# Strassen steps added in three units, two joins given to transfers, and another order of the branch units, in a one-core decoder block

## The chip, the cores and the metric

The kernel runs on one core of a Trainium2 chip. Its engines are TensorE (PE: matmuls, PEld: the weight loads that overlap them), VectorE (DVE), ScalarE (ACT), GpSimd (POOL, which here builds masks and issues transfers) and SyncE (SP, which only issues transfers). The metric is the device time of one execution in microseconds; "span" is the time from the first to the last instruction that the hardware profiler recorded.

## The reference

The block reads x (256 tokens × 4096 channels), normalizes it, multiplies it by one wide matrix and feeds two mixers, a causal pooling one and a gated short convolution. Each mixer's result goes through a branch matrix, is gated by a sigmoid, and the sum goes through an output matrix.

```python
h = rmsnorm(x, norm_w[l])
proj = jnp.einsum('bsd,de->bse', h, w_in[l])          # 4096 -> 20480
u_p, z_p, u_c, b_c, c_c, z_c, g_logit = jnp.split(proj, SPLIT_POINTS, axis=-1)
y_pool = causal_multiscale_pool(u_p, pool_w[l], pool_scale[l]) * jax.nn.silu(z_p)
y_conv = causal_gated_shortconv(u_c, b_c, c_c, conv_w[l], conv_b[l]) * jax.nn.silu(z_c)
ys = jnp.stack([y_pool, y_conv], axis=2)
br = jnp.einsum('bsnc,ncd->bsnd', ys, w_branch[l])    # 2 x (2048 -> 4096)
gates = jax.nn.sigmoid(g_logit.reshape(b, s, N_BRANCHES, d) + gate_b[l])
merged = jnp.sum(gates * br, axis=2)
x = x + jnp.einsum('bsd,de->bse', merged, w_out[l])   # 4096 -> 4096
return rmsnorm(x, final_norm_w)
```

## The kernel before

**Units and steps.** The work is a list of units, each of which makes 256 tokens × 1024 output columns. The eight units of the convolution come first (cz0, cb0, cu0, cc0, then the same with 1), then four of the pooling (pz0, pu0, pz1, pu1), eight of gate logits (g0_0 to g1_0), eight of the branch matrices (b0_0, b1_0, b0_1, ...; the first digit is the branch n, the second the column block c) and four of the output matrix (o0 to o3). A unit over x has 16 steps, one for each 256 input channels; a branch unit has 8. A step takes one 1 MB block of weights (256 channels × 1024 columns).

**Direct and Strassen steps.** Precision is kept by writing every fp32 operand as a high part, rounded to the matmul's format, and a low part, the rest; each product is three matmuls (high × high, high × low, low × high). A direct step, P, has 2 token halves × 2 column halves × 2 channel halves = 8 such products, 24 matmuls. A Strassen step, S, forms the sums of its weights' quarters on VectorE (tile `parts`) and needs 7 products, 21 matmuls. A string such as `"PPPPPSPSPSPSPSPS"` says which steps of a unit are which.

**What a step costs beside its matmuls.** SP loads the block into one of three `raw` buffers. ScalarE casts it to the high parts in a ring of 15 cells (`highs`, L58), VectorE subtracts to get the low parts (`lows`, L61). For an S step VectorE also adds the four weight sums, ScalarE casts them and VectorE subtracts once more (`added` and `split`). Up to `AHEAD = 4` steps are prepared ahead of the one that PE works on; a unit marked `urgent` sets this to its `lead` (2, or 3 for branch units) while its last step runs.

**The end of a unit.** Sums stand in eight PSUM banks: four `sums` banks (E) and four `shared` ones (F) that only S steps use. ScalarE copies each E bank out when its last matmul is done (`evacuate`, to E or Y) and each F bank to J. Where the unit has S steps, VectorE forms corner sums in J (`corner_sums`) and `combine` joins J to E: by a VectorE add, or, where the unit is marked `late`, by two accumulating transfers from the POOL queue (`gather`). The unit's epilogue `epi` is a list of items of which one runs for every six matmuls of the units behind it (`TICK = 6`).

**The order.** Everything is recorded in one pass and kept in program order on each engine, so an instruction waits for all that stands ahead of it on its engine. The queues of SP and POOL are filled in the same order.

**The first unit.** cz0 works while x is still being read and normalized: its 16 steps are all direct. VectorE and ScalarE each square one half of every block of rows (`square`), the scale of the tokens (`rin`) is known only near its end, and its E banks are copied to Y with that scale.

**The branch units.** b0_c leaves its product with the gates in Y, and b1_c multiplies by its own gates (`spare()`, the tile last_pair), adds Y, turns the sum by PE transposes (L462) and stores it to m_d for the output units. The operands of the branches (`y_ops`) are filled from y_d while earlier units run (`queue_fills`, `Fill`), in the order b0_0's, then b1_0's.

Of the kernel before, what the change touches and what calls it, by code (L numbers as in the profile page):

```python
# [31 lines left out]
TAIL = 3  # L32

SIX5 = "PPPPPSPSPSPSPSPS"
FIRST = (0, 1, 8, 2, 9, 3, 10, 11, 4, 12, 13, 5, 14, 6, 15, 7)
OPENED = 12
SEVEN3 = "PPPSPSPSPSPSPSPS"
NINE = "PSPSPSPSSPSPSSPS"
NINE_A = "PSPSSPSPSSPSPSPS"
NINE_P = "PSPSSPSPSSPSSPSP"  # L40
HOST = "PPBPPMMPSSPSSPSSPSS"
TEN = "PSPSSPSSPSSPSSPS"
OUT3 = "PSPSPSPSPSPSSPPP"
B0 = "PPPPSPSP"
B1 = "PSPSPSPP"
B1_FIRST = "PPSPSPSP"
B0_MORE = "PPPPSSPS"


@with_exitstack  # L50
def hybrid_block(ctx: ExitStack, tc: tile.TileContext, x, xc, prm, rows_in, w_in, pool_w, w_branch, w_out, out):
# [5 lines left out]
    def act(dst, src, func=AF.Copy, **kw):  # L57
        return pin(nc.scalar.activation(dst, src, func, **kw))  # L58
# [22 lines left out]
    def move(dst, src):  # L81
        return pin(nc.gpsimd.dma_start(dst, src))
# [36 lines left out]
    g_d = dram.tile([2, P, 2, NU], F32, name="g_d")  # L119
    side_d = dram.tile([2, P, 2, 4, P], F32R, name="side_d")  # L120
    y_d = dram.tile([2, 2, P, 4, 2, T], F32, name="y_d")
    m_d = dram.tile([4, P, 4, 2, T], F32, name="m_d")
    o_d = dram.tile([3, P, 2, NU], F32, name="o_d")

# [11 lines left out]
    def scale_col(b):  # L136
        return par[:, 96 + b:97 + b]

    opening = ExitStack()
    ctx.enter_context(opening)  # L140
    op = opening.enter_context(tc.tile_pool(name="opening", bufs=1))
# [313 lines left out]
    def transposes(src, done):  # L455
        items = []
        for j in range(4):
            def f(j=j):
                for i in range(2):
                    for t in range(2):  # L460
                        c = (2 * j + i) * P
                        pin(nc.tensor.transpose(shared(j)[:, i * T + t * P:i * T + (t + 1) * P],  # L462
                                                src[:, t, c:c + P], ident))
# [17 lines left out]
    def gap(n):  # L481
        return [None] * n
# [22 lines left out]

    def seq_x(text):
        if text is FIRST:
            return [("P", i) for i in FIRST]
        ns = text.count("S")
        if ns > NS + NB:  # L510
            ss = list(range(ND, 16)) + [resident[0]]
            if ns > NS + NB + 1:
                resident[0] = 2 * ND - 3 - resident[0]
                ss = [ss[-1]] + ss[:-1] + [resident[0]]
            ps = [i for i in range(ND) if i not in ss]
            return [(c, (ss if c == "S" else ps).pop(0)) for c in text]
        return sequence(text, ND, ND + NS + NB, NB)
# [4 lines left out]
    def in_unit(name, col, epi, text, **kw):  # L522
        units.append(Unit(name, lambda i: w_in[col // NU, i], seq_x(text), x_ops, epi, scaled=True, **kw))
        units[-1].text = text
        return units[-1]
# [12 lines left out]
            lambda: sub(side["tile"][:, 1], sa[:, 0:4], side["tile"][:, 0].bitcast(F32)),  # L538
            lambda: move(side_d[i - ND + 2], side["tile"])]

    def silu_y(late):
        def silu(t):
            act(Y[:, t], Y[:, t], AF.Silu, **(dict(scale=rin[:, t:t + 1]) if late else {}))
        return gap(18 if late else 3) + [lambda: silu(0), None, lambda: silu(1)]

    def rescale(d):
        return gap(18) + [lambda: act(d[:, 0], d[:, 0], scale=rin[:, 0:1]), None,
# [2 lines left out]
    def conv_units(c, first):  # L550
        base = 2 * HALF + c * NU

        def b_epi(u):
            def product(t):
                stt(E[:, t], E[:, t], rin[:, t:t + 1], Y[:, t], ALU.mult, ALU.mult)
            return gap(18) + [lambda: product(0), None, lambda: product(1), None, lambda: move(g_d[c], E)]

        def c_epi(u):
            def inner(j):
                if j == 3:  # L560
                    for i in range(4):
                        act(chan(E)[:, 2 * i:2 * i + 2], bankview(i))

            def outer(j):
                act(chan(J)[:, 2 * j:2 * j + 2], bankview(j))

            def taps(j):
                v, y = chan(E)[:, 2 * j:2 * j + 2], chan(Y)
                for i in range(2):
                    b = 2 * j + i  # L570
                    kb = 8 * c + b
                    act(y[:, b], v[:, i], AF.Identity, scale=tap_col(2, kb), bias=bias_col(kb))
                for s in (1, 2):
                    for i in range(2):
                        b = 2 * j + i
                        kb = 8 * c + b
                        stt(y[:, b, s:], v[:, i, 0:T - s], tap_col(2 - s, kb), y[:, b, s:], ALU.mult, ALU.add)

            items = [lambda: move(Y, g_d[c])] + gap(6) + pairs(transposes(E, inner)) + gap(5) + pairs(transposes(Y, outer))
            for j, n in enumerate((1, 7, 8, 8)):  # L580
                items += gap(n) + [lambda j=j: taps(j)]
            return items + [None, lambda: mul(chan(E), chan(J), chan(Y)), lambda: put(y_d[1, c], chan(E))]

        u = in_unit(f"cz{c}", base + 3 * HALF, lambda u: silu_y(u.late) + (gap(4) + side_items(ND - 1) + side_items(ND - 2) if first else []),
                    FIRST if first else SIX5, dst=Y)
        u.late = not first
        in_unit(f"cb{c}", base + HALF, b_epi, TEN if c else NINE_A).late = True
        u = in_unit(f"cu{c}", base, lambda u: rescale(Y), NINE, dst=Y)
        u.late = True
        in_unit(f"cc{c}", base + 2 * HALF, c_epi, NINE_A).urgent = lambda: mul(E, E, Y)  # L590

    def pool_units(c):
        u = in_unit(f"pz{c}", HALF + c * NU, lambda u: silu_y(True) + gap(4) + band_items(c), HOST if c else SIX5, dst=Y)
        u.late = True
        in_unit(f"pu{c}", c * NU, lambda u: [], NINE_P).urgent = lambda: None

# [113 lines left out]
    def spare():  # L710
        return last_pair["tile"].rearrange("p (a n) -> p a n", a=2)

    def branch_unit(n, c):
        def epi(u):
            if n == 0:
                if c:
                    return gap(10) + [lambda: move(spare(), gates_d[1, c])] + gap(8) + [lambda: mul(Y, E, Y)]
                return gap(8) + [lambda: mul(Y, E, Y)]
            turned = spare() if c < 3 else Y

            def gated():
# [12 lines left out]
            return gap(2) + [gated, None, lambda: add(E, E, Y), None,  # L734
                lambda: c < 3 and move(Y, gates_d[0, c + 1])] + gap(4) + pairs(transposes(E, copy)) + [stored]
# [362 lines left out]
    for u in units:  # L1098
# [28 lines left out]
        for st in u.steps:  # L1127
            assert st.prepared, (u.name, st.kind)
            run_step(u, st)
            if u.text is TEN and st.kind == "S" and st.op in x_ops[:ND] and st is not u.steps[-1]:  # L1130
                side_load(2 * ND - 3 - x_ops.index(st.op))
            state["now"] += 1
            if state["now"] == OPENED:
                opening.close()
                sums = ctx.enter_context(tc.tile_pool(name="parts", bufs=1)).tile([P, 4, NH], F32, name="parts")
# [111 lines left out]
```

## Time and profile before

| | us |
|---|---|
| median of 3 runs | 2357.35 (2356.61 to 2359.06) |
| the profiled execution | 2356.82 |
| its span | 2354.7 |
| busy: PE / PEld | 2340.7 / 1938.7 |
| busy: DVE / ACT / POOL | 2217.8 / 1542.9 / 139.0 |
| HBM read / written | 521.46 MB / 25.17 MB |

Busy times are sums of instruction durations of one engine. Matmuls overlap their neighbours' ends, so the pace of PE is read from starts, not from durations. TensorE had its full clock from about 10 us on; the mean over the span is 0.999. Unit starts, found by counting matmuls on PE: cz0 at 6.0, cb0 at 95.1, b0_0 at 1674.9, b1_0 at 1718.3, b0_1 at 1760.0, o0 at 2014.3 us of the span.

### The profile page before, as it was taken

How to read it: one execution, taken by the hardware profiler on the slowest of the kernel's cores; microseconds unless marked ns; L12 is line 12 of the kernel's file. 1: busy time of each engine (PE TensorE's matmuls, PEld its weight loads, DVE VectorE, ACT ScalarE, POOL GpSimd, SP SyncE). 2: the span in 40 equal slices, each digit the busy share in tenths (PEclk: the TensorE clock that was granted, in tenths of full speed). 3: DMA queues.
4: the chain of work that ended last, by engine and by line, in shares of the span. 5: the costliest groups of instructions: out<-in, count | busy, mean ns of one | idle time of the engine just before them, and what ended most of it. 6: DMA issues, size and time to landing. Idle time of an engine off the chain costs nothing.

```text
span 2354.7 us, 28337 instructions
## 1 busy us (share of the span) xinstructions
PE 2340.7 (99%) x10424; PEld 1938.7 (82%) x10424; DVE 2217.8 (94%) x2454; ACT 1542.9 (66%) x1841; POOL 139.0 (6%) x195
## 2 busy tenths in 40 slices
PE   9999999999999999999999999999999999999998
PEld 7888888888888888888888888888888888888886
DVE  8899989999979979979999999998999899999998
ACT  6666756766656666666677767677666566566664
POOL 0000000000001000100000000001101001000000
PEclk9999999999999999999999999999999999999999
DMA  9667655776656656656787787778767678767877
GB/s 351 231 234 248 217 201 215 251 232 233 222 207 216 219 196 213 220 198 222 242 258 254 256 265 246 250 267 283 258 225 247 254 247 282 250 206 263 260 255 279
DMA packets 95387, 569.44 MB, mean 242 GB/s; under 512 B 10320, under 2 KB 10576, under 8 KB 34832
## 3 DMA queue, kind: packets, MB, share of 16 engines
q1 hardware_dynamic: 69824, 485.39, 56.7%
q0 software_dynamic: 24848, 81.01, 13.7%
q8 instruction: 81, 1.33, 0.2%
q10 hardware_dynamic: 576, 1.24, 0.1%
q14 instruction: 58, 0.48, 0.1%
HBM read 521.46 MB, written 25.17 MB: 232 GB/s over the span
## 4 chain that ended last, share of the span: by engine, by line
PE 97%; DVE 1%; DMA 0%; ACT 0%; issue 0%; DVEq 0%; SPq 0%; ACTq 0%
PE sums L1026 70%; PE shared L1026 25%; PE shared L676 1%; PE shared L462 1%; DVE ring L61 1%; DMA raw<-in_w_branch_dram 0%; DVE parts L61 0%; DMA raw<-in_w_in_dram 0%; ACT ring L58 0%; DVE arena L61 0%; PE shared L652 0%; DVE J L61 0%; ACT E L58 0%; PE shared L653 0%; PE shared L655 0%
## 5 line engine op out<-in xcount | busy, mean ns | idle before, releaser
L1026 PE MATMUL sums<-ring,arena 128*128 128x512 f32 x7011 | 1640.7, 390 | 1.9 <-ACT E L58 1.1
L1026 PEld LDWEIGHTS sums<-ring,arena 128*128 128x128 f32 x7011 | 1315.3, 188 | 275.5 <-ACT E L58 1.5
L61 DVE TENSOR_TENSOR ring<-raw,ring 128x1024 fp32r<-128x1024 f32 (+2 forms) x887 | 962.2, 1104 | 70.4 <-ACT ring L58 69.5
L58 ACT ACTIVATE ring<-raw 128x1024 fp32r<-128x1024 f32 (+3 forms) x682 | 785.5, 1192 | 210.2 <-PE sums L1026 98.5
L58 ACT ACTIVATE ring<-parts 128x512 fp32r<-128x512 f32 (+1 forms) x683 | 510.4, 761 | 510.2 <-DVE parts L61 438.3
L1026 PE MATMUL shared<-ring,arena 128*128 128x512 f32 x2241 | 541.1, 389 | 0.0
L61 DVE TENSOR_TENSOR ring<-parts,ring 128x1024 fp32r<-128x1024 f32 (+1 forms) x475 | 524.5, 1146 | 8.7 <-ACT ring L58 8.7
L1026 PEld LDWEIGHTS shared<-ring,arena 128*128 128x128 f32 x2241 | 420.6, 188 | 87.3
L61 DVE TENSOR_TENSOR parts<-parts,raw 128x512 f32<-128x512 f32 x444 | 303.3, 683 | 0.0
L61 DVE TENSOR_TENSOR parts<-raw 128x1024 f32<-128x1024 f32 x222 | 270.2, 1217 | 10.9 <-DMA raw<-in_w_in_dram 6.0
L61 DVE TENSOR_TENSOR J<-J 128x512 f32<-128x512 f32 (+1 forms) x90 | 78.1, 868 | 6.0 <-ACT J L58 2.8
L1026 PE MATMUL sums<-ring,last_pair 128*128 128x512 f32 x306 | 76.2, 389 | 0.0
L58 ACT ACTIVATE J<-shared 128x512 f32<-128x512 f32 x128 | 69.5, 601 | 1.6
L1026 PEld LDWEIGHTS sums<-ring,last_pair 128*128 128x128 f32 x306 | 57.4, 188 | 11.9
L85 POOL DMA_DIRECT2D E<-J x28 | 34.2, 1463 | 479.5 <-ACT ring L58 300.1
L1026 PE MATMUL shared<-ring,last_pair 128*128 128x512 f32 x216 | 51.9, 389 | 0.0
L1026 PE MATMUL shared<-ring,side 128*128 128x512 f32 x207 | 50.7, 389 | 0.0
L1026 PEld LDWEIGHTS shared<-ring,last_pair 128*128 128x128 f32 x216 | 40.5, 188 | 8.4
L1026 PEld LDWEIGHTS shared<-ring,side 128*128 128x128 f32 x207 | 38.9, 188 | 8.1
L58 ACT ACTIVATE E<-sums 128x512 f32<-128x512 f32 x76 | 41.8, 592 | 4.5 <-PE sums L1026 2.7
L85 POOL DMA_DIRECT2D Y<-J x12 | 14.7, 1458 | 265.1 <-ACT ring L58 138.5
L58 ACT ACTIVATE E<-sums,rin 128x512 f32<-128x512 f32 x20 | 13.0, 689 | 13.9 <-PE sums L1026 13.9
(140 smaller groups left out, 645.6 us busy)
## 6 DMA issues: line engine op xcount, KB each, us to landing
raw<-in_w_in_dram SPq DMA_DIRECT2D x318, 1024.0 KB, 4.9
raw<-in_w_branch_dram SPq DMA_DIRECT2D x64, 1024.0 KB, 5.4
raw<-in_w_out_dram SPq DMA_DIRECT2D x64, 1024.0 KB, 4.8
E<-J POOLq DMA_DIRECT2D x28, 512.0 KB, 8.6
E<-in_rows_dram POOLq DMA_DIRECT2D x14, 512.0 KB, 9.8
Y<-J POOLq DMA_DIRECT2D x12, 512.0 KB, 9.3
gates_d<-E POOLq DMA_DIRECT2D x6, 1024.0 KB, 6.1
y_d<-E POOLq DMA_DIRECT2D x8, 512.0 KB, 5.2
```

The lines of the kernel that those rows point to most:

```text
L58: return pin(nc.scalar.activation(dst, src, func, **kw))
L61: return pin(nc.vector.tensor_tensor(out=dst, in0=a, in1=b, op=op))
L85: return pin(nc.gpsimd.dma_start(dst, src, accum_op=ALU.add))
L462: pin(nc.tensor.transpose(shared(j)[:, i * T + t * P:i * T + (t + 1) * P], src[:, t, c:c + P], ident))
L676: pin(nc.tensor.matmul(o, a, b, start=(k, i) == (0, 0), stop=(k, i) == (3, 2)))
L1026: pin(nc.tensor.matmul(ps, lhs, rhs, start=n == 0, stop=n == u.total[b] - 1))
```

## The change

In the first unit two of the sixteen steps (those with operands 14 and 15, the 13th and 15th in its order) become S, so the unit gets corner sums and is marked `late`: its join goes by two transfers, its scale moves from the copies to the silu (`silu_y`), and the preparation of the side operands runs beside the silu. Both halves of the squares go to ScalarE, and the tile of weight sums exists from the start. cb0 begins with three direct steps and keeps nine S. cz1 has seven S instead of six. cc0 and cc1 get a lead of 3 and other gaps between their items.

The branch units run b0_0, b0_1, b1_0, b1_1 and then by turns. All b0 units have three S steps (b0_0 had two) and are joined by transfers. b0_0's product with its gates is stored to the new DRAM tile p_d and Y is loaded with the gates of the next block; b1_0 loads the product back into J, where it is added to E.

```diff
 SIX5 = "PPPPPSPSPSPSPSPS"
+SEVEN5 = "PPPPPSPSSPSPSSPS"
 FIRST = (0, 1, 8, 2, 9, 3, 10, 11, 4, 12, 13, 5, 14, 6, 15, 7)
+FIRST_S = (14, 15)
+NINE_B = "PPPSSPSSPSSPSSPS"
 NINE_A = "PSPSSPSPSSPSPSPS"
-B0 = "PPPPSPSP"
 B1 = "PSPSPSPP"
-B1_FIRST = "PPSPSPSP"
-B0_MORE = "PPPPSSPS"
+B_LATE = "PPPPSSPS"
+B1_SECOND = "PPPPSSSP"
...
         if text is FIRST:
-            return [("P", i) for i in FIRST]
+            return [("S" if i in FIRST_S else "P", i) for i in FIRST]
...
-    def silu_y(late):
+    def silu_y():
         def silu(t):
-            act(Y[:, t], Y[:, t], AF.Silu, **(dict(scale=rin[:, t:t + 1]) if late else {}))
-        return gap(18 if late else 3) + [lambda: silu(0), None, lambda: silu(1)]
+            act(Y[:, t], Y[:, t], AF.Silu, scale=rin[:, t:t + 1])
+        return gap(18) + [lambda: silu(0), None, lambda: silu(1)]
...
-            items = [lambda: move(Y, g_d[c])] + gap(6) + pairs(transposes(E, inner)) + gap(5) + pairs(transposes(Y, outer))
+            items = [lambda: move(Y, g_d[c])] + gap(8) + pairs(transposes(E, inner)) + gap(3) + pairs(transposes(Y, outer))
...
-                    FIRST if first else SIX5, dst=Y)
-        u.late = not first
-        in_unit(f"cb{c}", base + HALF, b_epi, TEN if c else NINE_A).late = True
+        u = in_unit(f"cz{c}", base + 3 * HALF, z_epi, FIRST if first else SEVEN5, dst=Y)
+        u.late = True
+        in_unit(f"cb{c}", base + HALF, b_epi, TEN if c else NINE_B).late = True
...
-        in_unit(f"cc{c}", base + 2 * HALF, c_epi, NINE_A).urgent = lambda: mul(E, E, Y)
+        u = in_unit(f"cc{c}", base + 2 * HALF, c_epi, NINE_A)
+        u.urgent, u.lead = (lambda: mul(E, E, Y)), 3
...
             if n == 0:
-                if c:
-                    return gap(10) + [lambda: move(spare(), gates_d[1, c])] + gap(8) + [lambda: mul(Y, E, Y)]
-                return gap(8) + [lambda: mul(Y, E, Y)]
+                product = gap(18) + [lambda: mul(Y, E, Y)]
+                if c == 0:
+                    return product + [None, lambda: move(p_d, Y), lambda: move(Y, gates_d[0, 1])]
+                if c > 1:
+                    product[10] = lambda: move(spare(), gates_d[1, c])
+                return product
...
+            if c == 0:
+                head = [lambda: move(J, p_d.rearrange("p a (b n) -> p (a b) n", n=NH)), None, gated] + gap(4) + [
+                    lambda: add(quarters(E), quarters(E), J)] + gap(3)
+                rest = gap(7) + [lambda: move(spare(), gates_d[1, 1])]
+            return head + pairs(transposes(E, copy)) + [stored] + rest

-        text = (B1 if c else B1_FIRST) if n else B0_MORE if c else B0
+        text = B_LATE if n == 0 else B1_SECOND if c == 1 else B1
         u = Unit(f"b{n}_{c}", lambda i: w_branch[n, c, i], seq_y(text), y_ops[n], epi)
-        u.late = n == 0 and c > 0
+        u.late = n == 0
...
-    for c in range(4):
-        branch_unit(0, c)
-        branch_unit(1, c)
+    for n, c in ((0, 0), (0, 1), (1, 0), (1, 1), (0, 2), (1, 2), (0, 3), (1, 3)):
+        branch_unit(n, c)
...
-        act(q[:, 0], q[:, 0], AF.Square, accum_out=ssq[:, 0, c:c + 1])
-        stt(q[:, 1], q[:, 1], 1.0, q[:, 1], ALU.mult, ALU.mult, accum_out=ssq[:, 1, c:c + 1])
+        for t in range(2):
+            act(q[:, t], q[:, t], AF.Square, accum_out=ssq[:, t, c:c + 1])
```

Three places in the order of the engines follow, as the two programs were built (an engine's instructions in their order, destination <- source, shape).

ScalarE where cz0 ends and cb0 begins. `Y<-sums_81` to `_84` are the copies of the four E banks, `J<-shared` those of F, `ring<-raw` and `ring<-parts` casts of later steps. Before:

```order
L58 ACTIVATE ring<-raw 128x4x512
L58 ACTIVATE ring<-raw 128x3x512
L58 ACTIVATE ring<-parts 128x2x512
L58 ACTIVATE ring<-parts 128x512 x2
L58 ACTIVATE Y<-sums_82,rin 128x512
L58 ACTIVATE Y<-sums_84,rin 128x512
L58 ACTIVATE Y<-sums_81,rin 128x512
L58 ACTIVATE Y<-sums_83,rin 128x512
L58 ACTIVATE ring<-raw 128x2x512 x2
```

The change:

```order
L60 ACTIVATE J<-shared_85 128x512
L60 ACTIVATE J<-shared_87 128x512
L60 ACTIVATE ring<-raw 128x512
L60 ACTIVATE ring<-raw 128x3x512
L60 ACTIVATE J<-shared_86 128x512
L60 ACTIVATE J<-shared_88 128x512
L60 ACTIVATE ring<-raw 128x4x512
L60 ACTIVATE Y<-sums_82 128x512
L60 ACTIVATE Y<-sums_84 128x512
L60 ACTIVATE Y<-sums_81 128x512
L60 ACTIVATE Y<-sums_83 128x512
L60 ACTIVATE ring<-raw 128x3x512
```

Four copies of F banks are new, and a cast of a whole direct step (4x512) now stands right ahead of the E copies.

ScalarE where b0_0 ends (`E<-sums` are the copies of its E banks, `arena` the fills of branch operands). Before:

```order
L58 ACTIVATE J<-shared_86 128x512
L58 ACTIVATE J<-shared_88 128x512
L58 ACTIVATE ring<-raw 128x3x512
L58 ACTIVATE arena<-sb 128x512
L58 ACTIVATE E<-sums_82 128x512
L58 ACTIVATE E<-sums_84 128x512
L58 ACTIVATE E<-sums_81 128x512
L58 ACTIVATE E<-sums_83 128x512
```

The change:

```order
L60 ACTIVATE ring<-raw 128x2x512 x2
L60 ACTIVATE arena<-sa 128x512
L60 ACTIVATE E<-sums_83 128x512
L60 ACTIVATE ring<-raw 128x4x512
L60 ACTIVATE E<-sums_82 128x512
L60 ACTIVATE E<-sums_81 128x512
L60 ACTIVATE E<-sums_84 128x512
L60 ACTIVATE J<-shared_85 128x512
L60 ACTIVATE J<-shared_87 128x512
```

One E copy now comes early; the other three stand behind a cast of 4x512 in place of a cast of 3x512 and a fill.

POOL's queue over the first branch units (`E<-J` are the accumulating transfers of a join). Before:

```order
L82 DMA sa<-y_d 128x512
L82 DMA Y<-gates_d 128x2048
L82 DMA m_d<-last_pair 512x1x256 x2
L82 DMA sa<-m_d 128x512
L82 DMA sb<-m_d 128x512
L82 DMA sc<-m_d 128x512
L85 DMA E<-J 128x2x512 x2
L82 DMA last_pair<-gates_d 128x2048
```

The change:

```order
L84 DMA sa<-y_d 128x512
L87 DMA E<-J 128x2x512 x2
L84 DMA p_d<-Y 128x2048
L84 DMA Y<-gates_d 128x2048
L87 DMA E<-J 128x2x512 x2
L84 DMA J<-p_d 128x2048
L84 DMA m_d<-last_pair 512x1x256 x2
L84 DMA sa<-m_d 128x512
L84 DMA sb<-m_d 128x512
L84 DMA last_pair<-gates_d 128x2048
```

Two joins, the store of the product and its load are new ahead of the first m_d store; the load of b1_1's gates follows fills of the output operands, no join.

More of the change, by code (lines that the diff above doesn't have):

```diff
@@ L121, in hybrid_block @@
     y_d = dram.tile([2, 2, P, 4, 2, T], F32, name="y_d")
+    p_d = dram.tile([P, 2, NU], F32, name="p_d")
     m_d = dram.tile([4, P, 4, 2, T], F32, name="m_d")
@@ L137, in scale_col @@
         return par[:, 96 + b:97 + b]
+    sums = ctx.enter_context(tc.tile_pool(name="parts", bufs=1)).tile([P, 4, NH], F32, name="parts")
     opening = ExitStack()
@@ L582, in c_epi, with z_epi @@
             return items + [None, lambda: mul(chan(E), chan(J), chan(Y)), lambda: put(y_d[1, c], chan(E))]
-        u = in_unit(f"cz{c}", base + 3 * HALF, lambda u: silu_y(u.late) + (gap(4) + side_items(ND - 1) + side_items(ND - 2) if first else []),
-                    FIRST if first else SIX5, dst=Y)
-        u.late = not first
-        in_unit(f"cb{c}", base + HALF, b_epi, TEN if c else NINE_A).late = True
+        def z_epi(u):
+            items = silu_y()
+            if first:
+                sides = gap(8) + side_items(ND - 1) + side_items(ND - 2)
+                items = [lambda a=a, b=b: (a and a(), b and b()) for a, b in zip(items + gap(len(sides) - len(items)), sides)]
+            return items
+        u = in_unit(f"cz{c}", base + 3 * HALF, z_epi, FIRST if first else SEVEN5, dst=Y)
+        u.late = True
+        in_unit(f"cb{c}", base + HALF, b_epi, TEN if c else NINE_B).late = True
         u = in_unit(f"cu{c}", base, lambda u: rescale(Y), NINE, dst=Y)
         u.late = True
-        in_unit(f"cc{c}", base + 2 * HALF, c_epi, NINE_A).urgent = lambda: mul(E, E, Y)
+        u = in_unit(f"cc{c}", base + 2 * HALF, c_epi, NINE_A)
+        u.urgent, u.lead = (lambda: mul(E, E, Y)), 3
     def pool_units(c):
-        u = in_unit(f"pz{c}", HALF + c * NU, lambda u: silu_y(True) + gap(4) + band_items(c), HOST if c else SIX5, dst=Y)
+        u = in_unit(f"pz{c}", HALF + c * NU, lambda u: silu_y() + gap(4) + band_items(c), HOST if c else SIX5, dst=Y)
         u.late = True
@@ L733, in stored @@
                 merged[c] = now[0] + STORED
-            return gap(2) + [gated, None, lambda: add(E, E, Y), None,
-                lambda: c < 3 and move(Y, gates_d[0, c + 1])] + gap(4) + pairs(transposes(E, copy)) + [stored]
-        text = (B1 if c else B1_FIRST) if n else B0_MORE if c else B0
+            head = gap(2) + [gated, None, lambda: add(E, E, Y), None,
+                             lambda: c < 3 and move(Y, gates_d[0, c + 1])] + gap(4)
+            rest = []
+            if c == 0:
[4 more added lines that the diff above has]
+        text = B_LATE if n == 0 else B1_SECOND if c == 1 else B1
         u = Unit(f"b{n}_{c}", lambda i: w_branch[n, c, i], seq_y(text), y_ops[n], epi)
-        u.late = n == 0 and c > 0
+        u.late = n == 0
         if not u.late:
@@ L1134, in hybrid_block @@
                 opening.close()
-                sums = ctx.enter_context(tc.tile_pool(name="parts", bufs=1)).tile([P, 4, NH], F32, name="parts")
                 open_side()
```

## The prediction

> **What bounds the kernel now.** I read the page first: busy shares and the chain that ended last.
>
> ```profile
> span 2354.7 us, 28337 instructions
> PE 2340.7 (99%) x10424; PEld 1938.7 (82%) x10424; DVE 2217.8 (94%) x2454; ACT 1542.9 (66%) x1841; POOL 139.0 (6%) x195
> PE 97%; DVE 1%; DMA 0%; ACT 0%; issue 0%; DVEq 0%; SPq 0%; ACTq 0%
> ```
>
> TensorE is in 97% of the chain. A busy PE need not be a PE at its pace, so next come the waits of PE alone (engine, who it waited for, us in total, times, longest).
>
> ```profile
> PE shared L873 <- DVE warm L869: 1.1, 1, 1.1
> PE sums L1026 <- ACT E L58: 1.1, 1, 1.1
> PE sums L1026 <- DVE ring L774: 0.8, 1, 0.8
> ```
>
> Three waits in the whole program, two of them at the start, which the change does not touch. The pace stands in the timeline of PE (start, us, what, count).
>
> ```profile
> 67.92 16.48 PE L1026 MATMUL sums<-ring,arena 128*128 128x512 f32 x72
> 84.24 5.60 PE L1026 MATMUL sums<-ring,last_pair 128*128 128x512 f32 x24
> ```
>
> 72 matmuls from start to start take 84.24 − 67.92 = 16.32 us, **0.2267 us each**, and the next group follows at once. So the time is the number of matmuls at this pace plus 1.1 us of waiting in the middle. Whatever gives more than 1.1 us must remove matmuls; whatever costs must make PE wait.
>
> **Matmuls removed.** A direct step (P) is 8 groups of 3, 24 matmuls; a Strassen step (S) is 7 groups, 21. S rises by two in cz0, one in cz1 and one in b0_0; cb0, b1_0 and b1_1 are re-ordered with their counts kept. 4 × 3 = 12 matmuls, and the built program has 12 fewer, so that the change does what it says here is settled. 12 × 0.2267 = **−2.72 us**.
>
> **What the other engines pay.** The groups of VectorE kept apart by shape (busy us, mean ns):
>
> ```profile
> L61 DVE TENSOR_TENSOR ring<-raw,ring 128x1024 fp32r<-128x1024 f32 x530 | 632.9, 1217 | 14.4 <-ACT ring L58 14.1
> L61 DVE TENSOR_TENSOR ring<-parts,ring 128x1024 fp32r<-128x1024 f32 x413 | 487.2, 1216 | 8.7 <-ACT ring L58 8.7
> L61 DVE TENSOR_TENSOR parts<-parts,raw 128x512 f32<-128x512 f32 x444 | 303.3, 683 | 0.0
> L61 DVE TENSOR_TENSOR parts<-raw 128x1024 f32<-128x1024 f32 x222 | 270.2, 1217 | 10.9 <-DMA raw<-in_w_in_dram 6.0 <-DMA raw<-in_w_out_dram 4.8
> L61 DVE TENSOR_TENSOR ring<-raw,ring 128x512 fp32r<-128x512 f32 x298 | 201.2, 684 | 22.3 <-ACT ring L58 21.9
> L61 DVE TENSOR_TENSOR J<-J 128x512 f32<-128x512 f32 x60 | 41.4, 689 | 5.0 <-ACT J L58 2.8
> L61 DVE TENSOR_TENSOR J<-J 128x1024 f32<-128x1024 f32 x30 | 36.7, 1225 | 1.0
> L61 DVE TENSOR_TENSOR E<-E,J 128x2048 f32<-128x2048 f32 x5 | 11.4, 2287 | 1.0 <-ACT E L58 1.0
> ```
>
> And one square of the opening, from DVE's timeline:
>
> ```profile
> 33.29 1.22 DVE L73 SCALAR_TENSOR_TENSOR E<-E 128x1024 f32<-128x1024 f32 x1
> ```
>
> An S step on DVE is 1.22 + 2×0.68 + 0.68 + 1.22 + 2×1.22 = 6.9 us, a P step 2×1.22 = 2.4: **+4.5 us** for each step turned, +17.9 for four. cz0 now has corner sums (2×0.69 + 1.22 = 2.6); b0_0 gives its join to transfers (−2.3, the add E<-E,J); the four squares go to ACT (−4×1.22). Over the program DVE gains 17.9 + 2.6 − 2.3 − 4.9 = 13.3 us, and has 2354.7 − 2217.8 = 137 idle. That is an average; the stages decide.
>
> ```profile
> 50.00:95.10 45.10, 45.10 (x200) 37.35 (x199) 38.26 (x53) 26.12 (x31) 2.00 (x3) 1.00 0.77 282
> 1674.90:1718.30 43.40, 42.33 (x188) 34.72 (x186) 41.67 (x51) 31.21 (x39) 5.06 (x8) 1.00 0.80 263
> 1718.30:1760.00 41.70, 41.70 (x184) 34.51 (x185) 40.74 (x44) 27.32 (x34) 0.00 (x0) 1.00 0.55 202
> ```
>
> (Window, its length, then busy PE, PEld, DVE, ACT, POOL.) The second half of cz0 has 45.10 − 38.26 = 6.8 us of DVE idle; two S steps and the corner sums ask for 11.6, less 2.4 for the two squares that fall there. It runs 2.4 us over, 3.8 with the 1.4 us that PE saves, and eats into the preparation that stands up to four steps ahead; behind it three direct steps of cb0 give back 24×0.2267 − 2.4 = 3.0 us each. I cost DVE there at nothing; without that cover it is 3.8 us.
>
> **cz0 to cb0: a bank's copy behind a cast.** In the first pair of orders quoted with the change, ACT now has a 2048-wide cast ahead of the four copies out of PSUM. Before, they stood first:
>
> ```profile
> 89.68 12.40 PE L1026 MATMUL sums<-ring,arena 128*128 128x512 f32 x54
> 93.28 2.73 ACT L58 ACTIVATE Y<-sums,rin 128x512 f32<-128x512 f32 x4 [2.77 <-PE sums L1026]
> 95.91 2.00 ACT L58 ACTIVATE ring<-raw 128x1024 fp32r<-128x1024 f32 x2
> L58 ACT ACTIVATE ring<-raw 128x2048 fp32r<-128x2048 f32 x51 | 97.7, 1920 | 50.2 <-PE sums L1026 29.6 <-PE shared L676 12.8 <-DMA raw<-in_w_in_dram 4.8
> L58 ACT ACTIVATE E<-sums 128x512 f32<-128x512 f32 x76 | 41.8, 592 | 4.5 <-PE sums L1026 2.7
> ```
>
> The first bank of a closing P step is done 9 matmuls before the next unit writes it, 2.04 us. Its copy takes 0.59, and a matmul ends 16.48 − 16.32 = 0.16 after its slot, so the copy may start 2.04 − 0.16 − 0.59 = 1.3 us late, 1.2 with a hop between engines. A 1.92 us cast that starts as the bank closes makes PE wait 1.92 − 1.2 = 0.7. Ends: 0, if the cast is over by then, and 2.8, if its load also lands 2 us late. I take **+0.7**, since the cast waits on a load that follows a just freed buffer. The three copies behind it, and the next casts on ACT, move with it, no further stall.
>
> **End of b0_0.** This is the one wait of before:
>
> ```profile
> 1710.95 6.28 PE L1026 MATMUL sums<-ring,arena 128*128 128x512 f32 x27
> 1718.30 6.91 PE L1026 MATMUL sums<-ring,arena 128*128 128x512 f32 x29 [1.07 <-ACT E L58]
> 1715.76 1.49 ACT L58 ACTIVATE ring<-raw 128x1536 fp32r<-128x1536 f32 x1 [1.29 <-DMA raw<-in_w_branch_dram]
> 1717.15 0.61 ACT L58 ACTIVATE arena<-sb 128x512 fp32r<-128x512 f32 x1
> 1717.67 2.04 ACT L58 ACTIVATE E<-sums 128x512 f32<-128x512 f32 x4
> ```
>
> PE stood 1.07 us because the copies of E came behind a cast and a fill. The change makes this unit end with S, whose E banks close early, but the order shows three of the four copies behind a cast again, now 1.92 instead of 1.49 long. And DVE is fuller: 41.67 + 4.5 − 2.3 = 43.9 against 42.33 − 0.68 = 41.65 of matmuls, 2.2 over, while the window before had 1.7 idle. So: old wait −1.07; a wait for DVE of 0 to 2.2 (all of it hidden by preparation, or none), taken at 0.9, the nearer to the middle; a wait for the copy of 0 to 2.5 (cast and copy in full), taken at 1.07 + 1.92 − 1.49 = 1.5. Net **+1.3**, from −1.1 to +3.6. The wait before PE's next unit is where it would next be seen.
>
> **Product through DRAM.** The trace has no p_d; its nearest rows are 1 MB transfers on the same queue.
>
> ```profile
> E<-J POOLq DMA_DIRECT2D x28, 512.0 KB, 8.6
> gates_d<-E POOLq DMA_DIRECT2D x6, 1024.0 KB, 6.1
> Y<-gates_d POOLq DMA_DIRECT2D x3, 1024.0 KB, 5.6
> last_pair<-gates_d POOLq DMA_DIRECT2D x3, 1024.0 KB, 17.6
> 1762.17 2.28 DVE L61 TENSOR_TENSOR E<-E,J 128x2048 f32<-128x2048 f32 x1
> 1772.86 2.28 DVE L61 TENSOR_TENSOR E<-E,Y 128x2048 f32<-128x2048 f32 x1
> 1775.57 0.53 POOL L82 DMA_DIRECT2D Y<-gates_d  x1 [58.56 <-DVE E L61]
> 1775.60 1.03 PE L462 MATMUL shared<-ident,E 128*128 128x128 f32 x8
> ```
>
> The store has all of b0_1 (some 40 us) to land. The load is issued when the join has read J: in before b1_0 ends 183 matmuls behind 1718.30, near 1759.9, and that add runs from 2.3 to 4.6 us behind it. POOL issues 1775.57 − 1772.86 − 2.28 = 0.4 us after the DVE operation that it waits for; 5.6 to land and 2.3 for the add give 12.9 us, 15.2 if one more DVE operation of that size stands ahead. PE turns E 15.7 us behind the end in before, and one slot of six matmuls later now: 17.0. Hidden with 2 to 4 us to spare: **0**. The 17.6 row is issued right behind two gathers E<-J; in the POOL order no gather stands between the join and J<-p_d. At 17.6 PE would wait 24.9 − 17.0 = 8 us, 10 with the other operation.
>
> The branches behind, the gap changes of the conv units and cc0's longer lead move work under running matmuls: 0, with up to 1.0 at a boundary where copies meet a cast; I take **+0.3**.
>
> **Sum.** −2.72 + 0.7 + 1.3 + 0 + 0.3 = −0.4 on a span of 2354.7. That execution took 2356.82, 2.1 around its span; the runs have a median of 2357.35. 2357.35 − 0.4 = **2357.0**.
>
> **Rivals.**
>
> *All waits go.* PE keeps the saving and loses the old wait: −2.72 − 1.07 = −3.8, 2353.6. For it: only one wait stands in before. Against: the orders of ACT, where casts still precede copies. Chance 0.12.
>
> *J<-p_d lands late.* It takes the 17.6 us of last_pair<-gates_d, PE waits 8 to 10 us in front of b1_0's turn: 2365 to 2367. It decides from a landing of about 8 us. Against: no gather ahead of it. [...] Chance 0.06.
>
> *DVE sets the end.* Its added 13.3 us are paid in full: 2370.7, or some 2362 if only half. For it: 94% busy, and b0_0 runs over. Against: PE waited for DVE once in all, at the start. [...] Chance 0.08.
>
> **How the numbers follow.** Forecast 0.74, rivals 0.12, 0.06, 0.08. 0.2% is 4.7 us, about what a measurement can tell from none: below 2352.6 is faster, above 2362.1 slower. The first rival ends just short of it, so faster has only 0.06; slower has 0.06 of the late load, 0.05 of DVE and 0.02 of the forecast's own upper ends, 0.13; same 0.81. Range: from the first rival, 2353.6, to the upper ends of two of the three waits (+2.1, +2.3 on the forecast), 2361.4; the late load and DVE in full are left out.
>
> **What would show it.** PE x10412 in place of x10424. In the waits of PE: one of about 0.7 for Y behind cz0 near 94 us; near 1711 to 1716 one for DVE ring and one for ACT E, together over 2 us; none at L466 near 1815. Wrong: a PE wait of several us at L466 or for DVE ring in the first 100 us, or no wait at all in the middle, with the span below 2351.5.

## The result and the profile after

The change made the kernel slower: 2360.51 us (median of 20 runs, 2358.28 to 2363.23) against 2357.15 (20 runs, 2355.99 to 2360.21), a ratio of 1.0014, 95% interval 1.0008 to 1.0020. The forecast was 0.4 us faster; the measurement is 3.4 us slower. The profiled execution took 2360.47 with a span 4.0 us longer than before; it alone has a trace, so where the other nineteen lost their time is not shown.

The head of the page, and the waits of PE (who it waited for, us in total, times, longest):

```profile
span 2358.7 us, 28392 instructions
PE 2339.0 (99%) x10412; PEld 1935.5 (82%) x10412; DVE 2229.7 (95%) x2477; ACT 1551.5 (66%) x1870; POOL 143.9 (6%) x201
PE 94%; DVE 3%; ACT 1%; DMA 1%; issue 1%; SPq 0%; DVEq 0%; ACTq 0%
```

```profile
PE sums L1045 <- ACT E L60: 3.4, 2, 2.4
PE sums L1045 <- DVE ring L63: 2.3, 2, 1.7
PE sums L1045 <- ACT Y L60: 1.2, 1, 1.2
PE shared L892 <- DVE warm L888: 1.1, 1, 1.1
PE sums L1045 <- DVE ring L794: 0.7, 1, 0.7
```

The 12 matmuls are gone, and DVE has gained 2229.7 − 2217.8 = 11.9 us of work (13.3 forecast). PE's part of the chain fell from 97% to 94%, and the waits show why. Three of them were forecast: ACT Y near 94 us, one of the two for DVE ring, and one of the two for ACT E, both at the end of b0_0. The longest, 2.4 us for ACT E, was not.

Nor was the other wait for DVE ring, 1.68 us near 19 us (PE, the first unit, before and after):

```profile
5.98 16.55 PE L1026 MATMUL sums<-ring,arena 128*128 128x512 f32 x63 [0.83 <-DVE ring L774]
18.97 3.48 PE L1045 MATMUL sums<-ring,arena 128*128 128x512 f32 x14 [1.68 <-DVE ring L63]
```

It costs nothing against before. The next matmul behind the first 63 starts at 22.36 before and at 22.29 after, so they take 16.38 and 16.41 us: before, the first full clock on record is at 10.3 us, with 9 matmuls in the 3.41 us ahead of it and 16 in the 3.39 behind it; after, it is at 5.0 us, ahead of the first of the 63, and PE ran into the wait. The kernel of e10 below, with the first unit of before, has this wait too (1.69 us).

The timeline of PE places the others (start, us, what, count, idle before it and who ended it):

```profile
1705.17 7.87 PE L1045 MATMUL sums<-ring,arena 128*128 128x512 f32 x34
1713.67 0.73 PE L1045 MATMUL sums<-ring,arena 128*128 128x512 f32 x2 [0.63 <-DVE ring L63]
1714.24 2.89 PE L1045 MATMUL shared<-ring,arena 128*128 128x512 f32 x12
1718.14 7.16 PE L1045 MATMUL sums<-ring,arena 128*128 128x512 f32 x29 [1.01 <-ACT E L60]
...
1838.71 6.28 PE L1045 MATMUL sums<-ring,arena 128*128 128x512 f32 x27
1847.39 14.83 PE L1045 MATMUL sums<-ring,arena 128*128 128x512 f32 x57 [2.40 <-ACT E L60]
```

The last two rows are the end of b1_1 and the start of b0_2. At 0.2267 us each, the 27 matmuls from 1838.71 would hand over at 1844.83; the next group starts at 1847.39, 2.56 us late. That group is slow too: 57 matmuls need 57 × 0.2267 + 0.16 = 13.08 us and took 14.83, another 1.75. Together **4.3 us at one boundary**, about the whole loss of the span. The windows there (window, length, busy PE, PEld, DVE, ACT, POOL, granted clock, DMA share, GB/s) show both halves of it:

```profile
1840.00:1844.50 4.50, 4.50 (x22) 3.72 (x21) 4.01 (x5) 1.01 (x3) 0.00 (x0) 1.00 1.00 419
1844.50:1848.00 3.50, 1.09 (x6) 0.57 (x5) 1.11 (x1) 3.05 (x4) 0.00 (x0) 1.00 1.00 424
1848.00:1851.70 3.70, 3.70 (x11) 2.91 (x10) 3.44 (x3) 2.71 (x3) 0.00 (x0) 0.54 0.43 128
```

From 1840 to 1848 the 16 DMA engines show a busy share of 1.00, while up to 1844.5 ACT has next to nothing to do (1.01 of 4.50 us). Then the granted clock falls to 0.54: 11 matmuls in 3.7 us where 16 fit. What ACT was waiting for, from its timeline, and what POOL had issued, from POOL's:

```profile
1839.94 1.07 ACT L60 ACTIVATE J<-shared 128x512 f32<-128x512 f32 x2
1844.95 1.91 ACT L60 ACTIVATE ring<-raw 128x2048 fp32r<-128x2048 f32 x1 [3.93 <-DMA raw<-in_w_branch_dram]
1846.76 2.04 ACT L60 ACTIVATE E<-sums 128x512 f32<-128x512 f32 x4
```

```profile
1822.32 1.49 POOL L84 DMA_DIRECT2D m_d<-last_pair  x2 [16.79 <-ACT last_pair L60]
1832.14 0.56 POOL L84 DMA_DIRECT2D sa<-m_d  x1 [8.34 <-DMA m_d<-last_pair]
1832.69 0.56 POOL L84 DMA_DIRECT2D sb<-m_d  x1
1833.25 0.54 POOL L84 DMA_DIRECT2D last_pair<-gates_d  x1
1833.77 0.54 POOL L84 DMA_DIRECT2D sc<-m_d  x1
```

The landing of m_d releases three fills for o0 (256 KB each) and, between them in the queue, the 1 MB load of b1_1's gates: four transfers within two microseconds. The issues of DMA in windows of their own (KB, median us from issue to landing) give a weight load in the quiet stretch from 1780 to 1830, and the one issued at 1835, right behind the burst:

```profile
raw<-in_w_branch_dram SPq DMA_DIRECT2D x9, 1024.0 KB, 4.8
J<-p_d POOLq DMA_DIRECT2D x1, 1024.0 KB, 5.5
...
raw<-in_w_branch_dram SPq DMA_DIRECT2D x1, 1024.0 KB, 9.6
```

The load takes 9.6 us in place of 4.8. Its cast stands ahead of the four E copies in ACT's order, so the copies start when the weights have landed, and PE waits for a bank whose last matmul was done near 1842.8 (nine matmuls ahead of 1844.83), 4 us before its copy began. (The second row is the load of the product through DRAM, 5.5 us: no wait came of it.)

**Theory T**: the burst makes the weight load late, the cast passes that on to the copies, PE pauses, and the pause costs it its clock. **Rival S**: b1_1 has its three Strassen steps in a row, so DVE and ACT are late there whatever the transfers do.

### The profile page after: what moved, and what is told of

The parts are those of the page before. It is cut to its first block, busy times and chain, and to the rows that moved or that the text cites. A ratio compares the mean times of both kernels' runs of the same rounds, so it can differ in the third digit from the quotient of the medians.

```text
span 2358.7 us, 28392 instructions
## 1 busy us (share of the span) xinstructions
PE 2339.0 (99%) x10412; PEld 1935.5 (82%) x10412; DVE 2229.7 (95%) x2477; ACT 1551.5 (66%) x1870; POOL 143.9 (6%) x201
## 4 chain that ended last, share of the span: by engine, by line
PE 94%; DVE 3%; ACT 1%; DMA 1%; issue 1%; SPq 0%; DVEq 0%; ACTq 0%
PE sums L1045 67%; PE shared L1045 25%; DVE ring L63 1%; PE shared L687 1%; PE shared L466 1%; ACT ring L60 1%; DMA raw<-in_w_in_dram 1%; DMA raw<-in_w_branch_dram 0%; DVE sa L63 0%; DVE parts L63 0%; DVE arena L63 0%; ACT E L60 0%; DVE arena L75 0%; DVE arena L794 0%; PE shared L663 0%
## 5 line engine op out<-in xcount | busy, mean ns | idle before, releaser
L63 DVE TENSOR_TENSOR ring<-raw,ring 128x1024 fp32r<-128x1024 f32 (+3 forms) x896 | 966.4, 1100 | 71.6 <-ACT ring L60 70.3
L60 ACT ACTIVATE ring<-parts 128x512 fp32r<-128x512 f32 (+1 forms) x696 | 520.6, 760 | 547.9 <-DVE parts L63 478.6
L1045 PE MATMUL shared<-ring,arena 128*128 128x512 f32 x2277 | 549.7, 389 | 0.0
L63 DVE TENSOR_TENSOR ring<-parts,ring 128x1024 fp32r<-128x1024 f32 (+1 forms) x483 | 535.9, 1156 | 7.0 <-ACT ring L60 7.0
L1045 PEld LDWEIGHTS shared<-ring,arena 128*128 128x128 f32 x2277 | 427.4, 188 | 88.8
L63 DVE TENSOR_TENSOR parts<-parts,raw 128x512 f32<-128x512 f32 x452 | 312.7, 692 | 0.0
L63 DVE TENSOR_TENSOR parts<-raw 128x1024 f32<-128x1024 f32 x226 | 276.9, 1225 | 6.6 <-DMA raw<-in_w_out_dram 5.2
L60 ACT ACTIVATE E<-E 128x1024 f32<-128x1024 f32 x20 | 20.9, 1045 | 3.5 <-DMA E<-in_x_dram 3.5
```

The costliest lines, as they stand in the source:

```text
L63: return pin(nc.vector.tensor_tensor(out=dst, in0=a, in1=b, op=op))
L1045: pin(nc.tensor.matmul(ps, lhs, rhs, start=n == 0, stop=n == u.total[b] - 1))
```

## Experiments

The changed kernel was not run again beside the experiments. The kernel before was: 2357.04 us with e1 to e4, 2356.87 with e5 to e8 and 2356.73 with e9 to e11, against 2357.15 in the result above. So a difference to the changed kernel is good to some 0.4 us.

### e1: the gate load left out

Against the changed kernel:

```diff
-                rest = gap(7) + [lambda: move(spare(), gates_d[1, 1])]
+                rest = []
```

> This kernel leaves out the load last_pair<-gates_d of the second pair (1 MB), so b1_1 is gated with what the buffer held. Theory T (transfers): the three fills and this load, issued together at 1832 to 1834, make the weight load of 1835.25 take 9.59 us instead of about 5; so without it that load lands in 5 to 6.5 us, PE does not wait at the end of b1_1 (2.57 us before), the clock stays at 1.00 behind it, and the time falls by 2.6 + 0.3 of wait and some 1.5 of half clock, from 2360.5 to about 2356.1. Theory S (three Strassen steps in a row in b1_1 leave DVE and ACT late, the transfers only happen to be there): the wait of 2 to 3 us before b0_2 stays and the time stays at 2360 to 2361.

Measured: 2357.05 us (2356.53 to 2359.10, 11 runs); before on that chip 2357.04. The weight load of 1835 landed in 7.0 us, and PE ran through the boundary (timeline of PE, one group of 75 from b1_1 into b0_2):

```profile
1836.26 2.88 PE L1045 MATMUL shared<-ring,arena 128*128 128x512 f32 x12
1838.98 17.32 PE L1045 MATMUL sums<-ring,arena 128*128 128x512 f32 x75
```

75 × 0.2267 + 0.16 = 17.16: no wait, no half clock. S is out as a sufficient cause, since the three Strassen steps in a row are still there. The landing is 0.5 us above what T said, and the time 0.9.

### e2: the gate load earlier

Nothing is left out here; the turned sum of b1_0 goes to J, so last_pair is free as soon as b1_0 is gated.

```diff
-            turned = spare() if c < 3 else Y
+            turned = J if c == 0 else spare() if c < 3 else Y
...
-                head = [lambda: move(J, ...), None, gated] + gap(4) + [
+                head = [lambda: move(J, ...), None, gated, lambda: move(spare(), gates_d[1, 1])] + gap(3) + [
...
-                rest = gap(7) + [lambda: move(spare(), gates_d[1, 1])]
```

> Nothing is left out: b1_0's turned sum goes to J, so the load of the second pair's gates starts right behind the gating of b1_0, some 15 us earlier, outside the burst of fills. Theory T: wait before b0_2 gone, clock 1.00 there, 2356.1 (between 2355.5 and 2357.5; the upper end if the load now makes a weight load late elsewhere). Theory S: 2360 to 2361 with the wait where it was.

Measured: 2356.54 us (2355.72 to 2359.29, 11 runs), 4.0 below the changed kernel. POOL's and ACT's timelines:

```profile
1810.48 0.56 POOL L84 DMA_DIRECT2D last_pair<-gates_d  x1 [4.73 <-PE sums L1044]
```

```profile
1842.62 1.92 ACT L60 ACTIVATE ring<-raw 128x2048 fp32r<-128x2048 f32 x1 [1.39 <-DMA raw<-in_w_branch_dram]
1844.45 2.04 ACT L60 ACTIVATE E<-sums 128x512 f32<-128x512 f32 x4
```

The load is issued 23 us earlier (15 expected), the weight load takes 7.0 us, the cast waits 1.39 us in place of 3.93, and the copies start 2.3 us sooner, just in time. The same work at another moment gives the 4 us back.

### e3: the fills later

The other half of the burst is moved, the 1 MB load stays.

```diff
-                merged[c] = now[0] + STORED
+                merged[c] = now[0] + STORED + (20 if c == 0 else 0)
```

> Nothing is left out: the three fills sa, sb, sc of the first output unit (256 KB each) go behind the two gate loads on POOL's queue, the 1 MB load stays where it was. Theory T, sum of bytes: 1 MB instead of 1.75 MB beside the weights, the weight load takes 6 to 8 us, the wait before b0_2 falls under 1 us and the half clock with it: 2356 to 2357.5. Theory T', the 1 MB load alone is the cause: weight load still 9 us, 2360. Theory S: 2360 to 2361.

Measured: 2356.76 us (2355.93 to 2359.50, 11 runs). No wait before b0_2; the weight load that its copies hang on took 6.6 us. So taking away either 0.75 MB or 1 MB of the burst is enough: neither part alone makes the load late enough, and T' falls. (That the bytes alone matter is not shown: the 1 MB load also left 3.2 us ahead of the weight load here, and 2.0 us ahead in the changed kernel.) The profiled execution took 2359.06, 2.3 above that median, and shows where; PE behind cz0, and the windows (length, busy PE to POOL, granted clock, DMA share, GB/s):

```profile
96.50 19.56 PE L1045 MATMUL sums<-ring,arena 128*128 128x512 f32 x78 [2.12 <-ACT Y L60]
```

```profile
94.00:97.00 3.00, 0.88 (x3) 0.42 (x2) 2.93 (x4) 3.00 (x5) 0.00 (x0) 0.94 0.78 325
97.00:100.00 3.00, 3.00 (x9) 2.31 (x8) 3.00 (x3) 2.28 (x3) 1.85 (x3) 0.50 0.79 330
```

Here the forecast wait for Y is 2.12 us instead of 1.2, and it too is followed by half clock: 78 matmuls took 19.56 us, 1.7 more than 78 × 0.2267 + 0.16.

### e4: one Strassen step less in b1_1

```diff
-B1_SECOND = "PPPPSSSP"
+B1_SECOND = "PPPPSPSP"
```

> b1_1 takes two Strassen steps instead of three (PPPPSPSP), three matmuls more (+0.68 us), the transfers stay as they are. Theory T: the weight load issued near 1835 still takes 8 to 9.6 us; with one Strassen step less the preparation stands further ahead and the wait is between 0 and 1.5 us, 2356.8 to 2359. Theory S: the loads are no matter; the wait goes whatever they take: 2356.8.

Measured: 2358.60 us (2358.07 to 2361.86, 11 runs). The wait before b0_2 is gone although the transfers are as thick as in the changed kernel (windows):

```profile
1840.00:1844.50 4.50, 4.50 (x21) 3.75 (x20) 3.60 (x4) 4.33 (x6) 0.00 (x0) 1.00 1.02 430
```

but the three weight loads issued from 1832 to 1843.5 landed in 6.0 us (median), against 8.2 in the changed kernel, so T missed there: a step that needs less preparation also shifts when each load is issued. The last load that landed ahead of the boundary was issued at 1833.52, ahead of the 1 MB load at 1834.33, and took 7.1 us; the casts in front of the copies had no wait for it. So the burst alone does not make the wait: it takes a weight load issued behind it whose cast stands ahead of the copies. S expected no wait here either, so against S this run says nothing; e1 to e3 do. The time stayed 1.7 above 2360.5 − 4.3 + 0.7; 1.2 of that is a wait that came up elsewhere (PE where o0 ends and o1 begins):

```profile
2095.80 0.61 PE L1045 MATMUL sums<-ring,arena 128*128 128x512 f32 x2
2097.42 1.88 PE L1045 MATMUL sums<-ring,arena 128*128 128x512 f32 x7 [1.00 <-DVE arena L63]
```

### e5: the wait behind cz0

```diff
+        if first:
+            u.urgent, u.lead = (lambda: None), 2
```

(for cz0 alone: its closing copies go ahead of later preparation.)

> Beside after, cz0 is marked urgent with a lead of two, so that no 2048-wide cast stands ahead of the four copies of Y at its end; all else as after. My reading of the 1.2 us wait near 94 us (the copies stand behind the cast): it goes, and 1.2 to 1.4 us with it, from 2360.5 to about 2359.1. Rival: the preparation that is held back makes PE wait for DVE or ACT in the first steps of cb0 instead; 2360 to 2361.

Measured: 2358.93 us (2357.19 to 2361.34, 11 runs), 1.6 below the changed kernel, or 1.3 when each is taken against before in its own runs. The wait for Y is not in its list of waits; the one before b0_2 is, and longer (2.97 us). The weight load that it hangs on took 10.2 us, where the changed kernel's took 9.6: both waits are 7.2 us shorter than their load, and in e1 and e2, with the same steps and a load of 7.0 us, there is none. Why this load was slower is not shown; the burst and the boundary both came 0.4 us earlier.

### e6: two Strassen steps in b0_0

```diff
-        text = B_LATE if n == 0 else B1_SECOND if c == 1 else B1
+        text = "PPPPSPPS" if (n, c) == (0, 0) else B_LATE if n == 0 else B1_SECOND if c == 1 else B1
```

> Beside after, b0_0 takes two Strassen steps instead of three (PPPPSPPS), three matmuls more (+0.68 us). Reading of the prediction (the end of b0_0 costs 0.9 us of wait for DVE and 1.5 for the copies of E): both go, -2.4 + 0.7 = -1.7, 2358.8. Rival (DVE is behind anyway, the stall only moves): the wait before b0_2 grows by what was saved or DVE waits come later, 2360 to 2361.

Measured: 2360.18 us (2358.88 to 2364.81, 11 runs). The end of b0_0 is smooth (one group of 40, then 12, then 20, no idle time), so the prediction's two waits are what the third step costs. But the time falls by 0.3, not 1.7 (by 0.05 when each is taken against before in its own runs), so the time is that of the rival. Its mechanism is shown in part: the wait at o1 is back (1.00 us for DVE arena, as in e4), and the wait for Y behind cz0 is 1.79 us instead of 1.20. The one before b0_2 did not grow; it is 1.62 us, and the granted clock has a mean of 0.999 over the span (0.997 in the changed kernel). But the trace is that of the fastest of the eleven runs (2358.88), so it does not say what the median one lost there.

### e7 and e8: the fixes together

> The early load of the second pair's gates (e2) and cz0's lead (e5) together. If the two costs add: 2356.5 - 1.3 = 2355.2. If freeing the first makes a later stall: 2356.5.

> The same with two Strassen steps in b0_0 (e6). If all three add: 2356.5 - 1.3 - 1.7 = 2353.5, which would beat the kernel before by 3.5 us. If the saving of b0_0 is lost to later stalls of DVE near 2010 to 2100: 2355 to 2356.

Measured: 2355.17 us (2354.95 to 2356.14, 11 runs) and 2355.07 (2354.65 to 2357.06, 11 runs), before on that chip 2356.87 (33 runs, lowest 2356.05). No edit is new in them. The first two costs add, to a tenth of a us of what was expected, which is closer than runs on different chips allow (before differs by up to 0.4 us between them); the third does not, as e6 said, and the second kernel's trace has the wait at o1 (1.01 us). The ratio of the first is 0.9993, interval 0.9984 to 1.0002, so the interval alone does not exclude no gain, though 10 of its 11 runs lie below every run of before. Its PE at the two mended places (timeline):

```profile
88.70 11.52 PE L1046 MATMUL sums<-ring,arena 128*128 128x512 f32 x50
...
1837.68 21.79 PE L1046 MATMUL sums<-ring,arena 128*128 128x512 f32 x95
```

Both groups run across the boundary without a bracket: of the middle of the program only the cost of b0_0 is left.

### e9, e10 and e11: each half alone

The first kernel is before with the edits of the conv units (cz0, cb0, cz1, the squares, the gaps, cc0's lead), the second before with those of the branch units and p_d, the third the second with the early gate load.

```diff
# first: as changed, but the branch units of before
-    for n, c in ((0, 0), (0, 1), (1, 0), (1, 1), (0, 2), (1, 2), (0, 3), (1, 3)):
-        branch_unit(n, c)
+    for c in range(4):
+        branch_unit(0, c)
+        branch_unit(1, c)
...
# second: as changed, but the conv units of before
-        u = in_unit(f"cz{c}", base + 3 * HALF, z_epi, FIRST if first else SEVEN5, dst=Y)
+        u = in_unit(f"cz{c}", base + 3 * HALF, lambda u: silu_y(u.late) + (gap(4) + side_items(ND - 1) + side_items(ND - 2) if first else []),
+                    FIRST if first else SIX5, dst=Y)
...
# third: the second, and the edit of e2
```

> Only the first part of the change: the first conv unit, cb0, cz1, the squares, the gaps and cc0's lead; the branch units stay as in before. 9 matmuls fewer, -2.04; the wait for Y near 94 us +1.2 to +1.4, cz1 to cb1 +0.25: before minus 0.3 to 0.6, near 2356.6. If the 4.4 us of after do not come from the branches, this kernel shows them: above 2360.

> Only the other part: the order of the branch units, their texts and the product through DRAM; the first unit as in before. 3 matmuls fewer, -0.68; before's wait at the end of b0_0 goes, -1.34; two waits there, +2.4; the wait before b0_2 with the half clock behind it, +4.4: 4.8 above before, near 2361.7. Rival: without the first part the units stand 0.3 us later against the loads and the wait before b0_2 is smaller: 2358 to 2360.

> As the run with the branch part alone, with the second pair's gates loaded right behind the gating of b1_0 (the edit of e2). The 4.4 us go: -0.68 - 1.34 + 2.4 = 0.4 above before, near 2357.3. If the order of the units itself costs more than the burst: above 2359.

Measured (11 runs each, before on that chip 2356.73): 2358.81, 2360.86 and 2358.33 us, ratios 1.0010 (1.0001 to 1.0019), 1.0019 (1.0011 to 1.0028) and 1.0005 (0.9997 to 1.0014). The first was expected at 2356.6 and missed by 2.2. Its PE, behind cz0 and at o1:

```profile
96.05 18.00 PE L1038 MATMUL sums<-ring,arena 128*128 128x512 f32 x78 [1.88 <-ACT Y L62]
...
2096.87 1.88 PE L1038 MATMUL sums<-ring,arena 128*128 128x512 f32 x7 [0.99 <-DVE arena L65]
```

The wait for Y is 0.7 longer than in the changed kernel, and the wait at o1 appears, about 1.2 us from start to start. It appears in the six profiles whose Strassen steps differ from before by one or three (10421 or 10415 matmuls), and in none of the seven with 10424 or 10412. The order of DVE differs there. In the first of the three kernels the sum of a fill, `arena<-sa`, runs behind the preparation of a direct step (the row of 2.43 us), in before ahead of it (DVE's timelines):

```profile
2093.39 2.43 DVE L65 TENSOR_TENSOR ring<-raw,ring 128x1024 fp32r<-128x1024 f32 x3 [0.28 <-ACT ring L62]
2095.73 1.08 DVE L65 TENSOR_TENSOR arena<-sa,arena 128x896 fp32r<-128x896 f32 x1
```

```profile
2092.07 1.08 DVE L61 TENSOR_TENSOR arena<-sa,arena 128x896 fp32r<-128x896 f32 x1
2093.07 2.35 DVE L61 TENSOR_TENSOR ring<-raw,ring 128x1024 fp32r<-128x1024 f32 x2
```

Where the ring stands after an odd number of steps is my guess for the reason; it was not tried. So the parts are not worth the same alone as together, by 1 to 2 us, and these runs say only this much: the second half alone is 4.1 us slower than before, and moving one load in it takes back 2.5 (60% of it). In its profile the wait before b0_2 is 1.77 us and the clock stays full, as the rival said; the time, 2360.86, is 0.9 above the rival's all the same, and e11 is 1.0 above its forecast. Both have the wait at o1 (1.05 us), which neither expectation had.

## Why the prediction was wrong

**12 matmuls, −2.72.** Right: 10412.

**cz0 to cb0, +0.7.** Right in kind (the copies of Y behind a cast), too small. Undoing it gave 1.3 to 1.6 (e5), and 1.2 to 1.4 on top of e2 (e7), the lower figures against before in the same runs. ACT in the changed kernel:

```profile
91.64 1.08 ACT L60 ACTIVATE J<-shared 128x512 f32<-128x512 f32 x2
92.59 1.93 ACT L60 ACTIVATE ring<-raw 128x2048 fp32r<-128x2048 f32 x1
94.39 2.07 ACT L60 ACTIVATE Y<-sums 128x512 f32<-128x512 f32 x4
```

I let the cast start as the bank closes. cz0's last group starts at 88.25, so its first bank closed at 88.25 + 24 × 0.2267 − 2.04 = 91.65; but then two of the new copies of F banks ran, and the cast began 0.94 later. By the same sum that makes 0.94 + 1.92 − 1.2 = 1.7; PE's own starts give 95.05 − 93.69 = 1.4. The F copies were in the order that I quoted, without a price. The range, 0 to 2.8, held it.

**End of b0_0, +1.3.** Right. From start to start PE lost 1713.67 − (1705.17 + 34 × 0.2267) = 0.79 to DVE (0.9 taken) and 1718.14 − (1714.24 + 12 × 0.2267) = 1.18 to the copies, with some 0.3 in the matmuls behind (1.5 taken); before lost 1718.30 − (1710.95 + 27 × 0.2267) = 1.23. The 1.5 kept a fill of 0.61 us ahead of the copies that the quoted order no longer has there; without it the same sum gives 0.9, so that the size came out is in part luck.

**Product through DRAM, 0.** Right: the load took 5.5 us, 5.6 taken, and no wait stands at the transposes.

**"The branches behind, the gap changes of the conv units and cc0's longer lead move work under running matmuls: 0, with up to 1.0 at a boundary where copies meet a cast; I take +0.3."** This is the step that failed. The mechanism named there, copies behind a cast, is the one that came, but at 4.3 us in place of 0.3: 2.56 of wait and 1.75 of half clock. I bounded it by a cast whose load is on time. The load was 4.8 us late, because the change had put the 1 MB of b1_1's gates into the queue between o0's fills. The order I quoted showed exactly that, and I read it only for what would delay the gate load itself, not for what the gate load would delay. e1, e2 and e3 show it: without either part of the burst the wait is gone, and the time is 2356.5 to 2357.1, about where the rest of the sum as measured (−2.72 + 1.4 + 1.0 on 2357.15, which is 2356.8) puts it.

**The clock.** I priced no pause of the forecast for the clock, as the longest then known was 1.1 us, and behind that one, ahead of b1_0 in before, the clock stayed at 1.00 (1718.3 to 1760.0). Here it fell to 0.50 for 3.41 us behind a pause of 2.40 us, which cost another 1.75 us.

**The rivals.** DVE as the bound did not come: PE lost under 1 us to DVE in the middle. Its 11.9 us of extra work was hidden but for that. The prediction said that the change does not touch the waits at the start; a new one for DVE did come there (1.68 us near 19 us), but at no loss against before. Nor did all waits go, and J<-p_d was not late: the load that came late was one that no rival named.

## What to carry to other kernels

When a change moves a transfer, ask what the transfer will delay, not only what delays it: list what the same event releases, add up the bytes (1.75 MB here, and a weight load of 9.6 us in place of 4.8), and look which weight load is issued just behind, and what stands behind its cast. Copies out of PSUM that close a unit must not stand behind a cast that waits for a load: here that cast waited 3.93 us and PE 2.40. The pauses of 2.12 us (e3) and 2.40 us cost some 1.7 us more by the clock, and behind that of 1.77 us (e10) the clock stayed at 1.00, so price a pause of TensorE with the clock, and look at a saving in a kernel this full as worth nothing until the boundary that it moves has been checked.

## What the runs showed of the hardware

**The clock behind short pauses.** Behind pauses of 2.12 us (e3), 2.40 (the changed kernel) and 2.97 (e5) the granted clock was at half for 3.4 us, and the matmuls there took 1.7 to 1.8 us longer. Behind 1.68 (the changed kernel, near 19 us), 1.77 (e10) and 1.88 (e9) it was not. Early in cz0 it was at half behind 1.83 us in e8 (the timeline of PE), and not behind 1.83 us at the same place in e1, e3 and e4:

```profile
19.98 5.07 PE L1046 MATMUL sums<-ring,arena 128*128 128x512 f32 x14 [1.83 <-DVE ring L63]
```

14 matmuls need 3.33 us and took 5.07. So the length of a pause alone does not tell them apart; how much of it falls into one stretch of a grid does. In every profile the recorded changes of the granted clock lie whole multiples of 3.413 us apart: half clock begins 540 of them behind the first change in the changed kernel and in e5, 27 in e3 and 5 in e8, and ends one later. On that grid PE was idle for 1.83 (e8), 1.97 (e5), 2.12 (e3) and 2.40 us (the changed kernel) of the 3.41 us ahead of each fall. In all other stretches of the thirteen profiles, from the first change to the last matmul, it was idle for 1.77 us at most (e10). The pause of e9 puts 1.70 us into one stretch, those of e1, e3 and e4 1.40 at most. Windows cut on the grid (length, busy PE to POOL, granted clock, DMA share, GB/s): two of the changed kernel, the one ahead of the fall in e8, two of e10:

```profile
1844.82:1848.23 3.41, 1.00 (x5) 0.69 (x5) 1.34 (x1) 3.28 (x5) 0.00 (x0) 1.00 0.94 396
1848.23:1851.64 3.41, 3.41 (x10) 2.67 (x9) 3.15 (x3) 2.48 (x3) 0.00 (x0) 0.50 0.42 120
...
18.04:21.45 3.41, 1.58 (x7) 1.24 (x7) 3.41 (x4) 3.02 (x5) 0.00 (x0) 1.00 1.08 402
...
1844.60:1848.01 3.41, 1.64 (x7) 1.05 (x6) 2.52 (x2) 3.24 (x4) 0.00 (x0) 1.00 1.01 428
1848.01:1851.42 3.41, 3.41 (x16) 2.82 (x15) 3.41 (x3) 2.51 (x4) 0.00 (x0) 1.00 0.42 123
```

So in these thirteen profiles half clock follows each stretch with 1.83 us or more of idle PE and none with 1.77 or less, and the pause of 1.88 us that straddles two stretches (e9) left the clock at full. That the idle time within a stretch is the cause is my reading of them; no run changed it alone.

**A weight load beside another queue's transfers.** A weight load of 1 MB on SP's queue went from 4.8 to 9.6 us while POOL's queue held 1.75 MB; beside 0.75 MB it took 7.0 (e1, e2), beside the 1 MB load alone 6.6 (e3). From 1832 to 1843.5 the packets of POOL's queue took 43.6% of the time of the 16 transfer engines and those of SP's 44.0%; in e1 they took 20.7% and 66.9%. How the engines choose between the two queues is not shown.
